# Where attention scores and gating stand in the instruction order of a hybrid encoder

## The chip, the core and the metric

The kernel runs on one core of one Trainium2 chip. A core has engines that each run their own instructions in order: TensorE (PE in the profile, its weight loads PEld), VectorE (DVE), ScalarE (ACT), GpSimd (POOL) and SyncE (SP, which here issues most of the weight transfers). An instruction that waits holds up all that stands behind it on its engine. The metric is the device time of one execution in microseconds (us), as the median of several runs.

## The reference

Two layers (DEPTH = 2) on 256 tokens with 1024 channels, all in float32. Each layer normalises x, projects it once into all its inputs, and runs two mixers next to each other:

```python
for l in range(DEPTH):
    h = rmsnorm(x, norm_w[l])
    proj = h @ w_in[l]
    (q_a, k_a, v_a, ab_a, z_a, q_b, k_b, v_b, z_b,
     gate_a, gate_b) = jnp.split(proj, SPLIT_IDX, axis=-1)
    y_a = gated_delta_branch(q_a, k_a, v_a, ab_a, z_a, ...)
    y_b = diff_attention_branch(q_b, k_b, v_b, z_b, cos, sin, ...)
    merged = (jax.nn.sigmoid(gate_a) * (y_a @ w_pa[l])
              + jax.nn.sigmoid(gate_b) * (y_b @ w_pb[l]))
    x = x + merged @ w_out[l]
return rmsnorm(x, final_norm_w)
```

Branch b is differential attention with 8 heads. Each head has two sets of queries and keys of 64 channels. Two softmaxes p[0] and p[1] are taken, `a = p[0] - lam * p[1]` is multiplied by v, the result is normalised by its root mean square, weighted and multiplied by `silu(z_b)`. Branch a is a gated delta rule that runs over the tokens in both directions, in chunks: it needs a small triangular system solved for each chunk and head, and passes a state from chunk to chunk. Its output is normalised and gated by `silu(z_a)`.

## The kernel before

**Products.** Every product of the 256 tokens with a weight matrix is made in pieces of 512 columns. The weights come from HBM in four transfers of 512 KB per piece (index kp, 256 rows each; tile `raw_<name>`). ScalarE rounds each to a high part (`hi_<name>`, line 251), and VectorE subtracts to get the low part (`lo_<name>`, line 253). These two steps are called casts here. TensorE then makes three matmuls per 128 rows of weights (index kt, 0 to 7) and token half: high by high, high by low, low by high (lines 266 to 268). So a kt is 6 matmuls, and a piece 48. There are two buffers each for the high and the low part and three for the raw weights, so a cast can run only when TensorE is done with the cast two before it.

**Stages of a layer.** First v_b, then the convolved k, q and v of branch a, the q and k of branch b (`qk`), then the pieces zb0, zb1, za0, za1 (z of the two branches), gb0, gb1, ga0, ga1 (the merge gates), pb0, pb1 (branch b's output projection), pa0, pa1 and the output. Other work is put between these products:

- During zb0 to za1, the attention heads 0 to 7. `scores(h, after)` makes for each of two query tiles (qt) and two halves (n = 1, then n = 0) one product of 64 rows by 256 columns (line 913; in fp32, so two matmul instructions each, tile `sc`). The half n = 0 reads rows 0 to 63, n = 1 rows 64 to 127. Each half has its own PSUM bank; heads 2 to 7 share the two banks of one pool. VectorE takes the maxima (`mx`, line 920), ScalarE the exponentials (`es`, line 922), and VectorE combines the two softmaxes (lines 925 to 928). `attend(h, es, at, after)` transposes the result on TensorE (tile `at`, line 939) and multiplies by v (tile `av`, line 946). It gets its own two pins. On VectorE the same stretch holds `substitute`, the solution of the triangular systems step by step (lines 722 and 723), which is pinned to casts.
- During gb0 and gb1, the last head's attention, four products of keys and queries with their weighing by decays (`weigh_q`: `kq` on TensorE, line 653, then line 685 on VectorE), and the first merges of the triangular blocks (lines 775 to 821).
- After gb's casts are traced: the scales of branch b's output (`rb`, with a power on GpSimd, line 157) and `gated` for branch b. For four blocks (column piece i, token half m) `gated` makes four multiplications on VectorE (line 1026) and then transposes and splits the block (`split_T`; tile `pt_yb`, then `ybT`), which is the input of pb.
- During ga and pb, `chunks`, the passing of the state: `ktm` is scaled on VectorE (line 850), then products `sp`, `ks`, `y2p`, `qs`, `po`. `key_sums` (lines 888 to 899) sums the squares of the queries, with a way through DRAM, behind the last weighing.

**Order.** The order of the instructions on each engine is drawn up by a scheduler with a model of the times, not by the order of the source. It takes what is ready, by priority. What the source adds are pins: inside `with behind(x)` each instruction that runs on the same engine as x is queued after x. That is an order of issue alone, not a wait for x to end. In `scores` only the first product (qt = 0, n = 1) is pinned; the other three are kept behind it in program order. The pins of TensorE are given as places, a running count of kt over the pieces: 0 to 7 in zb0, 8 to 15 in zb1, 16 to 23 in za0, 24 to 31 in za1, 32 to 39 in gb0, 40 to 47 in gb1, 48 to 55 in ga0, 56 to 63 in ga1:

```python
names = [f"{nm}{l}{i}" for nm in ("zb", "za", "gb", "ga", "pb") for i in range(2)]
place = lambda at: mark["done", names[at // KT], at % KT]
```

So `place(5)` is the last matmul of zb0's sixth kt. `mark[name, kp]` holds the two casts of a piece's transfer, high and low; `[1]` is the low one, on VectorE.

Of the kernel before, what the change touches and what calls it, by code (L numbers as in the profile page):

```python
# [12 lines left out]
ALU = mybir.AluOpType  # L13
# [4 lines left out]
P = 128  # L18
# [3 lines left out]
NM = SEQ // P  # L22
# [27 lines left out]
def hybrid_encoder(  # L50
# [53 lines left out]
    mark = {}  # L104
# [45 lines left out]
    def heads4(ap):  # L150
        return ap.rearrange("p (h e) -> p h e", e=P)
# [72 lines left out]
    def behind(ins):  # L224
        return nullcontext() if ins is None else tc.issue_after(ins)
# [138 lines left out]
    for l in range(DEPTH):  # L364
# [463 lines left out]
        def chunks(g):  # L828

            U = U_[:, g]  # L830
            h0 = 4 * g
            hs4 = slice(h0, h0 + 4)

            def four(nm, lhs, rhs):
                ps = (bank if g else bank_c)(f"{nm}{l}{g}")
                for j4 in range(4):
                    with behind(mark["pin"]):
                        T.matmul(ps[:, j4 * P : (j4 + 1) * P], lhs(j4), rhs(j4), start=True, stop=True)
                return ps

            y1 = [A[:, g, d] for d in range(2)]
            st = [ktm[:, d, hs4, :] for d in range(2)]
            y2 = [vtm[:, 1 - d, hs4, :] for d in range(2)]
            for d in range(2):
                ps = four(f"y1p{d}", lambda j: U[:, tix(d, d, j), :], lambda j: vtm[:, d, h0 + j, :])
                S.copy(flat(y1[d]), ps)
            yield
            for d in range(2):
                with behind(mark[f"gb{l}1", 1][1]):
                    V.tensor_tensor(st[d], st[d], last(kds[:, d, hs4], P), ALU.mult)  # L850
                ps = four(f"sp{d}", lambda j: st[d][:, j, :], lambda j: y1[d][:, j, :])
                S.copy(flat(st[d]), ps)
            yield
            for d in range(2):
                cs = 1 - d
                ps = four(f"ks{d}", lambda j: kq[:, h0 + j, cs, 0, :], lambda j: st[d][:, j, :])
                for j4 in range(4):
                    V.scalar_tensor_tensor(y2[d][:, j4, :], ps[:, j4 * P : (j4 + 1) * P],
                                           nE[:, 2 * d + cs, h0 + j4 : h0 + j4 + 1],
                                           y2[d][:, j4, :], ALU.mult, ALU.add)  # L860
            yield
            for d in range(2):
                cs = 1 - d
                ps = four(f"y2p{d}", lambda j: U[:, tix(d, cs, j), :], lambda j: y2[d][:, j, :])
                S.copy(flat(y2[d]), ps)
                ps = four(f"qs{d}", lambda j: kq[:, h0 + j, cs, 1, :], lambda j: st[d][:, j, :])
                for j4 in range(4):
                    S.activation(osb(g, cs)[:, j4, :], ps[:, j4 * P : (j4 + 1) * P], AF.Copy,
                                 scale=E_[:, 2 * d + cs, h0 + j4 : h0 + j4 + 1])
                yield  # L870
            for c in range(NM):
                po = (bank if g else bank_c)(f"po{l}{g}{c}")
                for j4 in range(4):
                    for d in range(2):
                        yy = y1[d] if d == c else y2[d]
                        with behind(mark["pin"]):
                            T.matmul(po[:, j4 * P : (j4 + 1) * P], B[:, c, h0 + j4, d, :], yy[:, j4, :],
                                     start=d == 0, stop=d == 1)
                V.tensor_tensor(osb(g, c), heads4(po), osb(g, c), ALU.add)
                yield  # L880
# [51 lines left out]
        def attend(h, es, at, after):  # L932
            with tc.high_priority(offset=HP):
                ap_ = bank(f"at{l}{h}")
                aT = work.tile([P, NM, SEQ], F32, tag="w2a", name=f"aT{l}{h}", bufs=2)
                for qt in range(NM):
                    for kt in range(NM):
                        with behind(at):
                            T.transpose(ap_[:, kt * SEQ + qt * P : kt * SEQ + (qt + 1) * P],
                                        es[:, 0, qt, kt * P : (kt + 1) * P], ident)  # L940
                S.copy(aT.rearrange("p k q -> p (k q)"), ap_)
                op_ = bank(f"av{l}{h}")
                for qt in range(NM):
                    for kt in range(NM):
                        with behind(after):
                            T.matmul(op_[:, qt * P : (qt + 1) * P], aT[:, kt, qt * P : (qt + 1) * P],
                                     vb[h // 4][:, kt, h % 4 * P : h % 4 * P + P],
                                     start=kt == 0, stop=kt == NM - 1)
            oh = ob[h // 4][:, :, h % 4 * P : h % 4 * P + P]
            S.copy(oh, op_[:, :SEQ].rearrange("p (q e) -> p q e", q=NM))  # L950
            for qt in range(NM):
                S.activation(sqj[:, :P], oh[:, qt, :], AF.Square, accum_out=ssb[:, qt, h : h + 1])
# [50 lines left out]
        for p in range(4):  # L1003
            z_part((zb, za)[p // 2], (C_ZB, C_ZA)[p // 2], ("zb", "za")[p // 2], p % 2)
            for h in (2 * p, 2 * p + 1):
                es[h] = scores(h, place(4 * h))
                if h:
                    attend(h - 1, es[h - 1], place(4 * h + 1), place(4 * h + 3))
            substitute(names[p])
            if p == 0:  # L1010
                place_v(mark[f"zb{l}0", 0][0])
                place_v(mark[f"zb{l}0", 3][0])
            elif p == 1:
                place_v(mark[f"zb{l}1", 1][0])
# [3 lines left out]
        step(mg)  # L1018
        step(mg)

        def gated(o_, z_, r_, nw_, yT, nm, tiles=range(NM)):
            for i in range(2):
                for m in tiles:
                    zv, ov = heads4(z_[i][:, m, :]), o_(i, m)
                    for j in range(4):
                        V.scalar_tensor_tensor(ov[:, j, :], ov[:, j, :],
                                               r_[:, m, 4 * i + j : 4 * i + j + 1],
                                               zv[:, j, :], ALU.mult, ALU.mult)
                    split_T(yT[i], ov, m, f"{nm}{i}", w=nw_)

        def gate(c_base, nm, tag, between=(None, None)):
# [9 lines left out]
        def branch(yT, w_, gt, nm, places=(None,) * 4):  # L1041
            for i in range(2):
                def evac_p(m, ps, i=i):
# [3 lines left out]

        gtb = gate(C_GB, f"gb{l}", "ev",
                   (lambda: attend(7, es[7], place(33), place(35)),
                    lambda: [weigh_q(n // 2, n % 2, place((36, 38, 40, 41)[n])) for n in range(4)]))  # L1050
        r0 = small.tile([P, NM, NH], F32, tag="r0", name=f"r0{l}")
        V.reciprocal(r0, s_all[:, :, 0, :].rearrange("p h q -> p q h"))
        rb = small.tile([P, NM, NH], F32, tag="rb", name=f"rb{l}")
# [3 lines left out]
        V.scalar_tensor_tensor(rb, rb, 0.5 * (1.0 - lam0), r0, ALU.mult, ALU.mult)  # L1057

        ybT = pair(f"ybT{l}")
        gated(lambda i, m: heads4(ob[i][:, m, :]), zb, rb, nw[:, 1:2], ybT, f"yb{l}")  # L1060

        gta = gate(C_GA, f"ga{l}", "eo")
        branch(ybT, w_pb[l], gtb, f"pb{l}")
# [110 lines left out]
```

## Time and profile before

| what | us |
|---|---|
| median of 3 runs (772.15 to 773.23) | 772.15 |
| the profiled execution, its whole time | 775.43 |
| its span, first to last instruction | 773.7 |

The profile is of one execution. Its rows count from the span's start. An engine's busy time is the union of its instructions; matmuls overlap, and their ends are modelled, so the distance from one start to the next says more than a duration. The granted TensorE clock was 0.998 of full speed over the span. A row of the timeline or of a group of instructions gives the engine, the line in the kernel, the operation, the tiles written and read, the shapes and the count; what stands in square brackets is the idle time of the engine before it and who ended it. A row of the chain of waits gives start, duration, engine, tile and line of a piece of the chain that ended last.

### The profile page before, as it was taken

What the parts mean: (1) busy time and instruction counts of PE and PEld (TensorE: products, weight loads), DVE (VectorE), ACT (ScalarE), POOL (GpSimd) and SP (SyncE); (2) the same over time, 40 slices, a digit from 0 to 9 for tenths busy, and PEclk for the clock granted to TensorE, in tenths of its full rate; (3) what the DMA queues carried; (4) which work ended last, traced back from release to release, by engine and by line L of the source; (5) the groups of instructions that cost most, each with busy time, mean ns of one, the idle gap of its engine ahead of it and who ended that gap; (6) DMA issues with size and microseconds to landing.
All of it is one profiled execution on the core that took longest, in us unless ns stands there. A gap on an engine that the chain in (4) does not pass through costs nothing.

```text
span 773.7 us, 13772 instructions
## 1 busy us (share of the span) xinstructions
PE 756.6 (98%) x5158; PEld 643.9 (83%) x5158; DVE 577.7 (75%) x1083; ACT 471.9 (61%) x1012; POOL 125.9 (16%) x187
## 2 busy tenths in 40 slices
PE   7999999999999999999999999999999999999996
PEld 4899889977778789988889889888677878998884
DVE  5686899989876754487567779999989685527782
ACT  5657675567765664655545677555777746465541
POOL 5000441111123011000010025202110410301000
PEclk9999999999999999999999999999999999999999
DMA  7662767765469542356674258768554965323641
GB/s 238 219 188 71 223 196 209 224 183 177 126 193 219 168 137 87 108 161 226 212 224 137 83 148 262 206 178 235 158 164 116 218 212 166 112 83 110 218 136 54
DMA packets 71794, 131.24 MB, mean 170 GB/s; under 512 B 12287, under 2 KB 12751, under 8 KB 71728
## 3 DMA queue, kind: packets, MB, share of 16 engines
q1 hardware_dynamic: 62718, 111.94, 48.4%
q0 software_dynamic: 6304, 15.15, 7.4%
q10 hardware_dynamic: 2706, 3.28, 1.3%
q8 instruction: 40, 0.66, 0.4%
q14 instruction: 26, 0.21, 0.1%
HBM read 123.44 MB, written 6.91 MB: 168 GB/s over the span
## 4 chain that ended last, share of the span: by engine, by line
PE 75%; DVE 10%; DMA 9%; ACT 3%; issue 2%; POOL 1%; SPq 0%; POOLq 0%; DVEq 0%; ACTq 0%
PE pp_vb L306 4%; PE sc L913 3%; DMA raw_gb<-in_w_in_dram 2%; PE pp_qk L267 2%; PE pp_qk L268 2%; DMA raw_vb<-in_w_in_dram 2%; PE pp_qk L266 2%; PE pp_o L306 2%; PE pf_v L322 2%; PE pp_za L267 2%; PE pf_v L326 2%; PE pf_v L324 2%; PE pp_ga L268 2%; PE pp_ga L266 2%; PE pf_k L322 2%
## 5 line engine op out<-in xcount | busy, mean ns | idle before, releaser
L267 PE MATMUL pp_qk<-lo_qk,hT 128*128 128x512 f32 x128 | 50.7, 396 | 0.3
L268 PE MATMUL pp_qk<-hi_qk,hT 128*128 128x512 f32 x128 | 50.0, 391 | 0.0
L253 DVE TENSOR_TENSOR lo_qk<-raw_qk,hi_qk 128x1024 fp32r<-128x1024 f32 x32 | 39.8, 1243 | 9.7 <-ACT hi_qk L251 9.5
L251 ACT CAST hi_qk<-raw_qk 128x1024 fp32r<-128x1024 f32 x28 | 29.4, 1050 | 25.9 <-PE pp_qk L268 12.6
L266 PE MATMUL pp_qk<-hi_qk,hT 128*128 128x512 f32 x128 | 45.2, 393 | 0.0
L253 DVE TENSOR_TENSOR lo_pb<-raw_pb,hi_pb 128x1024 fp32r<-128x1024 f32 x16 | 19.6, 1224 | 26.3 <-ACT hi_pb L251 26.1
L324 PE MATMUL pf_q<-hT,hi_q 128*128 128x256 f32 x128 | 36.2, 286 | 0.0
L322 PE MATMUL pf_q<-hT,hi_q 128*128 128x256 f32 x128 | 36.1, 287 | 0.0
L322 PE MATMUL pf_v<-hT,hi_v 128*128 128x256 f32 x128 | 35.9, 285 | 0.0
L324 PE MATMUL pf_v<-hT,hi_v 128*128 128x256 f32 x128 | 35.8, 284 | 0.0
L322 PE MATMUL pf_k<-hT,hi_k 128*128 128x256 f32 x128 | 35.8, 285 | 0.0
L324 PE MATMUL pf_k<-hT,hi_k 128*128 128x256 f32 x128 | 35.7, 283 | 0.0
L326 PE MATMUL pf_q<-hT,lo_q 128*128 128x256 f32 x128 | 34.9, 285 | 0.0
L922 ACT ACTIVATE es<-sc,mx 128x256 f32<-128x256 f32 x64 | 29.7, 475 | 8.2 <-DVE mx L920 8.2
L326 PE MATMUL pf_v<-hT,lo_v 128*128 128x256 f32 x128 | 34.5, 288 | 0.0
L326 PE MATMUL pf_k<-hT,lo_k 128*128 128x256 f32 x128 | 34.3, 283 | 0.0
L551 DVE SCALAR_TENSOR_TENSOR cvq<-pf_q,cw,cvq 128x254 f32<-128x254 f32 (+1 forms) x64 | 29.9, 476 | 1.9 <-ACT cvq L547 1.4
L251 ACT CAST hi_pa<-raw_pa 128x1024 fp32r<-128x1024 f32 x16 | 16.9, 1054 | 23.2 <-PE pp_pa L268 17.0
L551 DVE SCALAR_TENSOR_TENSOR cvv<-pf_v,cw,cvv 128x254 f32<-128x254 f32 (+1 forms) x64 | 30.0, 480 | 0.1
L551 DVE SCALAR_TENSOR_TENSOR cvk<-pf_k,cw,cvk 128x254 f32<-128x254 f32 (+1 forms) x64 | 28.5, 479 | 2.0 <-ACT cvk L547 1.3
L267 PEld LDWEIGHTS pp_qk<-lo_qk,hT 128*128 128x128 f32 x128 | 24.0, 188 | 6.8 <-DVE lo_qk L253 2.0
L253 DVE TENSOR_TENSOR lo_ga<-raw_ga,hi_ga 128x1024 fp32r<-128x1024 f32 x16 | 19.4, 1223 | 12.7 <-ACT hi_ga L251 12.7
(362 smaller groups left out, 2525.4 us busy)
## 6 DMA issues: line engine op xcount, KB each, us to landing
raw_qk<-in_w_in_dram SPq DMA_DIRECT2D x32, 512.0 KB, 4.0
raw_k<-in_w_in_dram SPq DMA_DIRECT2D x16, 512.0 KB, 4.6
raw_q<-in_w_in_dram SPq DMA_DIRECT2D x16, 512.0 KB, 3.7
raw_v<-in_w_in_dram SPq DMA_DIRECT2D x16, 512.0 KB, 3.7
raw_zb<-in_w_in_dram SPq DMA_DIRECT2D x16, 512.0 KB, 3.8
raw_za<-in_w_in_dram SPq DMA_DIRECT2D x16, 512.0 KB, 3.7
raw_gb<-in_w_in_dram SPq DMA_DIRECT2D x16, 512.0 KB, 5.3
raw_o<-in_w_out_dram SPq DMA_DIRECT2D x16, 512.0 KB, 4.9
```

The costliest lines, as they stand in the source:

```text
L251: high = (V.tensor_copy if kp in turned else S.copy)(hi[:, :, :n], raw[:, :, :n]).ins
L253: mark[nm, kp] = high, V.tensor_tensor(lo[:, :, :n], raw[:, :, :n], hi[:, :, :n].bitcast(F32), ALU.subtract).ins
L266: T.matmul(o, act[kt // 4][:, 0, kt % 4, ts_], hi, start=kt == 0, stop=False)
L267: T.matmul(o, act[kt // 4][:, 0, kt % 4, ts_], lo, start=False, stop=False)
L268: mark["proj"] = T.matmul(o, act[kt // 4][:, 1, kt % 4, ts_], hi, start=False, stop=kt == KT - 1).ins
L306: mark["proj"] = T.matmul(o, a_, w_, start=kt == 0 and a_ is ah and w_ is hi, stop=kt == KT - 1 and a_ is al).ins
L322: T.matmul(o, hi[:, cs], act[kt // 4][:, 0, kt % 4, :], start=first, stop=False, skip_group_check=True)
L324: T.matmul(o, hi[:, cs], act[kt // 4][:, 1, kt % 4, :], start=False, stop=False, skip_group_check=True)
L326: T.matmul(o, lo[:, cs], act[kt // 4][:, 0, kt % 4, :], start=False, stop=done, skip_group_check=True)
L551: V.scalar_tensor_tensor(ca[:, o0:o1], acc[:, b, o0 + sft : o1 + sft], cw[:, j, cb : cb + 1], ca[:, o0:o1], ALU.mult, ALU.add)
L913: mm = T.matmul(sp[n][:, qt * SEQ : (qt + 1) * SEQ], qkT[h // 4][rows, 0, h % 4, qt * P : (qt + 1) * P], qkT[h // 4][rows, 1, h % 4, :], s ...
L922: S.activation(es[:, n, qt, :], spv[:, qt, :], AF.Exp, bias=mx[:, n, qt : qt + 1], accum_out=s_all[:, h, n, qt : qt + 1])
```

## The change

No instruction is added or removed. Four sets of pins change:

1. Scores of the heads 0 to 7: from the places 0, 4, 8, ..., 28 to 2, 6, 12, 15, 19, the last matmul of head 3's attention product (for head 5), that of head 4's (for head 6), and 31. To be able to name them, `attend` now records its last matmul in `mark["av", h]`.
2. `weigh_q`: from the places 36, 38, 40, 41 to 37, 41, 43, 45.
3. The scaling of `ktm` in `chunks(g)`: from behind the low cast of gb1's second transfer to behind the low cast of ga0's transfer g (0 or 1).
4. The gating of branch b, unpinned before: its four blocks go behind the low casts 1, 2, 3 and 3 of gb1. The pin holds the multiplications alone, not the transposes and splits after them. Branch a's gating, which uses the same function, stays unpinned.

```diff
@@ chunks
-                with behind(mark[f"gb{l}1", 1][1]):
+                with behind(mark[f"ga{l}0", g][1]):
                     V.tensor_tensor(st[d], st[d], last(kds[:, d, hs4], P), ALU.mult)
@@ attend
-                            T.matmul(op_[:, qt * P : (qt + 1) * P], aT[:, kt, qt * P : (qt + 1) * P],
+                            mark["av", h] = T.matmul(op_[:, qt * P : (qt + 1) * P], aT[:, kt, qt * P : (qt + 1) * P],
                                      vb[h // 4][:, kt, h % 4 * P : h % 4 * P + P],
-                                     start=kt == 0, stop=kt == NM - 1)
+                                     start=kt == 0, stop=kt == NM - 1).ins
@@ the z products
-                es[h] = scores(h, place(4 * h))
+                es[h] = scores(h, mark["av", h - 2] if h in (5, 6) else place((2, 6, 12, 15, 19, 0, 0, 31)[h]))
                 if h:
                     attend(h - 1, es[h - 1], place(4 * h + 1), place(4 * h + 3))
@@ gated
-        def gated(o_, z_, r_, nw_, yT, nm, tiles=range(NM)):
+        def gated(o_, z_, r_, nw_, yT, nm, tiles=range(NM), after={}):
...
-                        V.scalar_tensor_tensor(ov[:, j, :], ov[:, j, :],
-                                               r_[:, m, 4 * i + j : 4 * i + j + 1],
-                                               zv[:, j, :], ALU.mult, ALU.mult)
+                        with behind(after.get((i, m))):
+                            V.scalar_tensor_tensor(ov[:, j, :], ov[:, j, :],
+                                                   r_[:, m, 4 * i + j : 4 * i + j + 1],
+                                                   zv[:, j, :], ALU.mult, ALU.mult)
@@ gate gb
-                    lambda: [weigh_q(n // 2, n % 2, place((36, 38, 40, 41)[n])) for n in range(4)]))
+                    lambda: [weigh_q(n // 2, n % 2, place((37, 41, 43, 45)[n])) for n in range(4)]))
@@ the gating of branch b
-        gated(lambda i, m: heads4(ob[i][:, m, :]), zb, rb, nw[:, 1:2], ybT, f"yb{l}")
+        gated(lambda i, m: heads4(ob[i][:, m, :]), zb, rb, nw[:, 1:2], ybT, f"yb{l}",
+              after={(i, m): mark[f"gb{l}1", min(2 * i + m + 1, 3)][1] for i in range(2) for m in range(NM)})
```

## The prediction, made before the change was run

> **What bounds the kernel now.** I read the page first, then the chain of waits, then the timeline of the two stages in which the pins move.
>
> ```profile
> span 773.7 us, 13772 instructions
> PE 756.6 (98%) x5158; PEld 643.9 (83%) x5158; DVE 577.7 (75%) x1083; ACT 471.9 (61%) x1012; POOL 125.9 (16%) x187
> ```
>
> TensorE is the bound: it is idle for 773.7 - 756.6 = 17 us in all, and no instruction is added or taken away. A gain can come from two places only: from matmuls that take longer than they must (a busy PE row hides that), and from the idle time. So I looked for both where the diff moves work.
>
> The first is in the scores. These are the rows of the chain of waits (start, duration) for the z products of layer 1, with the attention products that stand next to them:
>
> ```profile
> 172.69 0.63 PE sc L913 x2
> ...
> 175.33 1.06 PE sc L913 x6
> ...
> 182.91 0.63 PE sc L913 x2
> ...
> 186.49 1.06 PE sc L913 x6
> ...
> 194.12 0.63 PE sc L913 x2
> ...
> 203.86 1.06 PE sc L913 x8
> ...
> 208.73 0.63 PE sc L913 x2
> ...
> 211.86 0.89 PE av L946 x8
> 212.75 1.06 PE sc L913 x6
> ...
> 219.43 0.89 PE av L946 x8
> 220.32 0.63 PE sc L913 x2
> ...
> 227.35 0.63 PE sc L913 x2
> ```
>
> A head has eight score matmuls: two query tiles, two halves n, each an fp32 product of two instructions. The halves use rows 64 to 127 and 0 to 63 of the array, and run side by side when they are issued together: head 4, in one piece, takes 1.06 us for eight. Where the first pair (n = 1 of query tile 0, the one that is pinned) is issued alone, it has no partner: 0.63 us for two, and the six that follow later take 1.06 all the same, since their last pair is alone too. Seven of eight heads are split like this, in both layers; a split costs **0.63 us** of TensorE.
>
> The second is a pair of waits in the product gb, for the low half of its weights:
>
> ```profile
>   PEld pp_gb L267: 3.2, 4
>   PE pp_gb L267: 1.9, 4
> ```
>
> These are the rows "who waited" of tile raw_gb: four waits, two in each layer, 1.9 us of idle PE (3.2 by its weight loads, which stop first).
>
> **Scores, head by head.** A pin cannot move a head to an earlier place, only hold its first pair back; the other six stay behind it. So I compare the new pin with where the two parts are now, counting the product's matmuls (six to a place).
>
> Head 1: first pair after place 4, the rest after 38 matmuls of zb0; new pin 42. Head 2: first pair after 62, rest after 74 of zb; new pin 78. Head 5: rest directly behind head 3's attention product at 211.86, which is the new pin. Head 7: rest after 92 of za, new pin 96. In these four the pin lies at or just behind the point at which the second part went out, so its PSUM bank is free by then and all eight go out together: 4 x 0.63 = 2.5 us per layer. Head 4's pin (24 matmuls of za) is where it stands now: 0. Head 3's (96 of zb) and head 6's (behind head 4's attention) are where their first pairs stand already, at 194.12 and 220.32; I take 0 for both, bounds 0 and -0.63 each.
>
> Head 0 is different. It merges too, but its two parts cost nothing today:
>
> ```profile
> 165.44 1.04 ACT L251 CAST hi_zb<-raw_zb 128x1024 fp32r<-128x1024 f32 x1
> ...
> 165.59 0.70 PE L913 MATMUL sc<-qkT 64*128 64x256 f32 x2
> ...
> 166.53 0.73 PE L266 MATMUL pp_zb<-hi_zb,hT 128*128 128x512 f32 x2 [0.25 <-ACT hi_zb L251]
> ...
> 166.76 1.22 DVE L253 TENSOR_TENSOR lo_zb<-raw_zb,hi_zb 128x1024 fp32r<-128x1024 f32 x1
> ...
> 167.19 1.13 PE L913 MATMUL sc<-qkT 64*128 64x256 f32 x6
> ...
> 168.25 0.50 PE L267 MATMUL pp_zb<-lo_zb,hT 128*128 128x512 f32 x1
> ```
>
> PE waits here for zb0's second pair of k-tiles: the high half ends at 166.48, the low half at 167.98. The scores fill both waits. Held back to place 2 (the third k-tile) they leave them empty: the low product can start some 0.2 us sooner, and then 1.06 + about 0.1 for the change of shape comes on top. I take **+0.9 us** per layer; bounds +1.2 (nothing gained at 168) and -0.6 (the scheduler finds other work for the gap).
>
> Together 0.9 - 2.5 = -1.6 us per layer, -3.2 for both. The later scores delay each head's softmax. That costs nothing while its transposes find products to run beside; every head has a z or gb product over it.
>
> **Gating, ktm and kq.** The same two waits in the timeline of layer 1:
>
> ```profile
> 242.49 2.94 POOL L157 TENSOR_TENSOR rb<-rspre,mhalf 128x16 f32<-128x16 f32 x1
> ...
> 247.71 0.17 DVE L1057 SCALAR_TENSOR_TENSOR rb<-rb,r 128x16 f32<-128x16 f32 x1
> ...
> 248.83 1.05 ACT L251 CAST hi_gb<-raw_gb 128x1024 fp32r<-128x1024 f32 x1 [1.77 <-DMA raw_gb<-in_w_in_dram]
> 248.93 3.76 DVE L1026 SCALAR_TENSOR_TENSOR ob<-ob,rb,zb 128x128 f32<-128x128 f32 x14
> ...
> 253.12 1.23 DVE L253 TENSOR_TENSOR lo_gb<-raw_gb,hi_gb 128x1024 fp32r<-128x1024 f32 x1
> ...
> 254.26 2.50 DVE L850 TENSOR_TENSOR ktm<-ktm,kds 128x512 f32<-128x512 f32 x4
> ...
> 254.40 0.50 PE L267 MATMUL pp_gb<-lo_gb,hT 128*128 128x512 f32 x1 [0.67 <-DVE lo_gb L253]
> ...
> 258.93 2.36 DVE L253 TENSOR_TENSOR lo_gb<-raw_gb,hi_gb 128x1024 fp32r<-128x1024 f32 x2
> ...
> 260.21 0.50 PE L267 MATMUL pp_gb<-lo_gb,hT 128*128 128x512 f32 x1 [0.47 <-DVE lo_gb L253]
> ```
>
> VectorE runs the 16 gatings in one block ahead of gb1's second cast, and the ktm scaling (4 instructions, 2.50 us) and two kq weighings ahead of the third and fourth. With the gatings queued behind casts 1, 2, 3 and 3 and ktm behind ga's casts, the casts go first and both waits go: -1.9 us for the layers together (bounds 0 and -3.2). What the moved work feeds comes later: gating feeds ybT, which pb reads when ga is done; ktm feeds this:
>
> ```profile
> L838 PE MATMUL sp<-A,ktm x32: 270/275/275, 286.3 to 290.2; 128*128 128x128 f32 x32
> ```
>
> From 256.8, the scaling's end, to 286.3 there are 29 us of cover. Head 7, now behind all of za, gives rb later than 247.88, by 2 to 3 us as an estimate (its own eight matmuls and the last four of za). The first gating is now behind the second cast of gb1, which can run from 249.88 to 251.1, when its high half is there; so VectorE has no wait for rb that PE would see. The kq groups keep their size, later by one to four places, each followed by its weighing on VectorE:
>
> ```profile
> 242.14 1.23 DVE L685 TENSOR_TENSOR B<-kq,B 128x1024 f32<-128x1024 f32 x1 [0.15 <-PE kq L653]
> ```
>
> One group (eight matmuls of the shape that takes 0.89 us in the av rows above) leaves the stretch before gb1 and head 7's scores (1.06) enter it, so PE reaches gb1's first cast no sooner than now. I take 0.
>
> **Sum.** -3.2 - 1.9 = -5.1 us. The profiled execution took 775.43 us (span 773.7), so 770.3 on its scale; it lies 3.3 above the median of the runs, 772.15, so **767.0 us** there. The forecast's own range: with heads 3 and 6 merged (-2.5) and all of the 3.2 waits gone, 772.15 - 8.9 = 763.2; with two merges, head 0 at 1.2 and half of the waits, about 771.
>
> **Rivals.** *Evacuation holds the gain* (0.15). Two banks of scores now land at once, and the maxima over them wait on VectorE:
>
> ```profile
> 170.00:178.00 8.00, 8.00 (x40) 5.74 (x39) 8.00 (x20) 6.08 (x17) 2.31 (x5) 1.00 0.65 206
> 178.00:186.00 8.00, 8.00 (x37) 6.22 (x36) 8.00 (x18) 6.60 (x17) 0.42 (x1) 1.00 0.59 173
> ...
> 262.00:266.00 4.00, 4.00 (x57) 3.34 (x48) 1.05 (x2) 3.30 (x7) 0.00 (x0) 1.00 0.66 238
> ```
>
> (Busy us of PE, weight loads, VectorE, ScalarE, POOL.) VectorE is full for 16 us from 170 on, so PE saved there could turn into waits for low halves. Then the merges give nothing, head 0 costs 1.8 and gb returns 1.9: 772 us, no change. Against it: in that stretch head 0 puts PE behind, not ahead. [...]
>
> *Key sums come late and block VectorE* (0.17), the slower side. They wait for the last kq weighing, now at gb1's sixth k-tile, and stand behind the gatings and ktm:
>
> ```profile
> 283.45 2.20 POOL L898 DMA_DIRECT2D qss<-qdr  x4 [1.46 <-DMA qdr<-qss]
> ...
> 289.02 0.26 DVE L899 TENSOR_REDUCE ssq<-qss 128x16 f32<-128x64 f32 x1 [5.37 <-DMA qss<-qdr]
> ...
> 293.44 0.17 DVE L1084 TENSOR_TENSOR rq<-rq 128x16 f32<-128x16 f32 x1 [2.82 <-POOL rq L1082]
> 294.16 1.12 DVE L858 SCALAR_TENSOR_TENSOR vtm<-ks,nE,vtm 128x128 f32<-128x128 f32 x4 [0.54 <-PE ks L838]
> ```
>
> VectorE already stands still for 5.37 us for that DMA and 2.82 us for POOL, and the updates of vtm, for which the chunk chain on PE waits, come 0.5 us behind. A shift of s us costs PE s - 0.5 per layer. From s = 3.1 it eats the whole gain (2 x 2.6 = 5.2); with s = 5, 767.0 + 9.0 = 776; with 4, 774. For it: 4.3 us of gating (16 x 0.27), 2.5 of ktm and two weighings of 1.23 move towards it. Against: from 262 to 266 VectorE is busy for 1.05 of 4 us, so there is room for them.
>
> *All splits go* (0.08): heads 3 and 6 merge and head 0 is hidden: 2 x 7 x 0.63 + 1.9 = 10.7, 761.4 us.
>
> **How the numbers follow.** Forecast 0.60, of which 0.06 is within 0.2% (about 1.5 us, what a measurement can tell here). Faster: 0.54 + 0.08 + 0.03 of the first rival = 0.65; same: 0.06 + 0.11 = 0.17; slower: 0.17 + 0.01 = 0.18. The range 763 to 775 holds the forecast, the first rival and the slower one up to s = 4.5, and leaves out most of the last.
>
> **What would show it.** Right: the chain of waits has score pieces of x8 at 1.06 for heads 1, 2, 5 and 7 and no x2 of 0.63 there; PE idles about 1.5 us at zb0's second cast; tile raw_gb has no wait of PE at L267; the maxima (L920) and exponentials (L922) keep their busy time. Wrong: x2 pieces still in number; new idle time of PE at L939, L946 or L838; the wait at L899 ends later relative to the ks products. What would break the forecast is the order of the instructions itself: the scheduler draws it anew for all engines, and a pin of a few matmuls can move work that the diff doesn't name.

## The result, and the profile after

The changed kernel takes **768.0 us** (median of 7 runs, 767.3 to 771.1), the kernel before 772.71 beside it (7 runs, 771.5 to 775.4): a ratio of 0.9947, 95% interval 0.9925 to 0.9969. That is 4.7 us less; 767.0 was forecast. Its profiled execution took 769.31 us. The tables below compare one execution of each kernel; that of before (775.43) lies 2.7 us above this median, that of after 1.3, so they differ by 6.1 us where the medians differ by 4.7.

The head of its page, beside the one shown of before (span 773.7, PE busy 756.6):

```profile
span 767.5 us, 13772 instructions
PE 748.7 (98%) x5158; PEld 640.6 (83%) x5158; DVE 576.9 (75%) x1083; ACT 470.1 (61%) x1012; POOL 125.8 (16%) x187
```

PE is busy 7.9 us less and idle 18.8 us instead of 17.1. To see where, both traces are cut at the same events: zb0's first matmul, gb0's first, gb1's last, ga1's last. The first three rows are layer 1, the others layer 2. The columns are busy us of PE, weight loads, VectorE, ScalarE, POOL, then the granted clock, DMA share and GB/s. Before:

```profile
162.70:232.00 69.30, 69.05 (x342) 51.89 (x342) 60.35 (x130) 50.36 (x138) 10.43 (x18) 1.00 0.57 163
232.00:266.60 34.60, 33.45 (x477) 27.75 (x476) 24.75 (x44) 20.88 (x47) 7.44 (x11) 1.00 0.80 200
266.60:310.00 43.40, 43.40 (x377) 38.81 (x376) 21.62 (x39) 26.05 (x48) 6.68 (x6) 1.00 0.38 115
539.80:609.60 69.80, 69.00 (x341) 51.86 (x340) 60.23 (x130) 50.43 (x138) 9.74 (x17) 1.00 0.57 162
609.60:644.00 34.40, 33.66 (x477) 27.86 (x476) 24.73 (x44) 20.98 (x47) 8.13 (x12) 1.00 0.80 200
644.00:687.40 43.40, 43.40 (x377) 38.82 (x376) 21.21 (x38) 25.77 (x47) 6.66 (x6) 1.00 0.36 113
```

After:

```profile
162.20:228.80 66.60, 64.28 (x338) 49.38 (x336) 59.52 (x129) 50.14 (x137) 8.61 (x16) 1.00 0.56 160
228.80:262.80 34.00, 33.02 (x473) 27.47 (x472) 21.54 (x39) 19.08 (x46) 10.22 (x13) 1.00 0.88 211
262.80:307.10 44.30, 44.30 (x386) 39.65 (x385) 25.27 (x45) 27.36 (x50) 5.76 (x6) 1.00 0.39 121
536.00:601.30 65.30, 63.97 (x338) 49.42 (x336) 59.42 (x129) 49.45 (x135) 9.16 (x16) 1.00 0.56 163
601.30:637.00 35.70, 34.41 (x473) 28.69 (x472) 21.71 (x39) 19.14 (x46) 9.69 (x13) 0.95 0.85 204
637.00:681.30 44.30, 44.30 (x386) 39.68 (x386) 24.77 (x44) 27.12 (x49) 5.76 (x6) 1.00 0.38 115
```

The z products are 2.7 and 4.5 us shorter, together 7.2, more than twice what the forecast had (3.2). The gate products give some of it back: gb and ga together were 78.0 and 77.8 us and are 78.3 and 80.0, so they lost 2.5 us where the forecast had them win 1.9. ga is longer by 0.9 and 0.8 because eight transposes of the gated output (`pt_yb`) moved there out of gb in each layer; gb in turn took in four transposes of head 6 (`at`), which stood at the end of z before and take 0.45 us where the chain of waits has four of them. The remaining 1.5 us of the span lie outside these windows.

**The scores.** The chain of waits of the kernel after, through zb and za of layer 1:

```profile
190.03 1.06 PE sc L913 x8
195.42 1.06 PE sc L913 x8
...
203.46 1.06 PE sc L913 x8
...
219.10 1.06 PE sc L913 x8
```

Not one piece of 0.63 is left: all eight heads of a layer go out in one piece, heads 3 (195.42) and 6 (219.10) too, whose pins had not seemed to move anything. PE's busy time in z falls by 4.8 and 5.0 us: seven splits at 0.63 are 4.4, and head 6's transposes are 0.45. The windows also show what it costs: PE's idle time in z is 2.3 and 1.3 us, before 0.25 and 0.8. In layer 1 most of it is at zb0's second cast, where head 0 used to stand (timeline of after):

```profile
165.69 0.73 PE L266 MATMUL pp_zb<-hi_zb,hT 128*128 128x512 f32 x2 [0.62 <-ACT hi_zb L251]
...
167.19 0.50 PE L267 MATMUL pp_zb<-lo_zb,hT 128*128 128x512 f32 x1 [0.76 <-DVE lo_zb L253]
...
168.32 1.13 PE L913 MATMUL sc<-qkT 64*128 64x256 f32 x8
...
187.94 1.16 PE L946 MATMUL av<-vb,aT 128*128 128x128 f32 x8 [0.67 <-ACT aT L941]
```

In layer 2 PE waits only 0.39 us there. The last row is a wait that came with the new order, for ScalarE's copy of head 1's transposed attention weights; in layer 2 it is 0.68 us.

**The gate products.** The rows of tile `raw_gb`, the raw weights of gb, for the kernel after: what its instructions waited for (in part), then which PE rows waited for them (us, times), then the time from issue to landing.

```profile
  DMA raw_gb<-in_w_in_dram: 11.6, 2
...
  PE pp_gb L267: 1.7, 3
...
  PE pp_gb L266: 0.5, 1
...
DMA to landing us min/median/max: 3.8/7.8/13.3
```

Before, PE waited 1.9 us at L267, and the landings were:

```profile
DMA to landing us min/median/max: 3.6/5.3/10.8
```

So the waits that were to go are still there, 2.2 us of them. But they are other waits. These are rows of the timeline of layer 1, all engines, first of the kernel before:

```profile
233.29 0.50 ACT L922 ACTIVATE es<-sc,mx 128x256 f32<-128x256 f32 x1
...
233.74 1.08 ACT L251 CAST hi_gb<-raw_gb 128x1024 fp32r<-128x1024 f32 x1
...
236.22 0.39 SPq L247 DMA_DIRECT2D raw_gb<-in_w_in_dram  x1
...
245.48 1.05 ACT L251 CAST hi_gb<-raw_gb 128x1024 fp32r<-128x1024 f32 x1 [3.92 <-DMA raw_gb<-in_w_in_dram]
```

And of the kernel after:

```profile
227.79 1.04 ACT L251 CAST hi_gb<-raw_gb 128x1024 fp32r<-128x1024 f32 x1
...
230.12 1.71 SPq L247 DMA_DIRECT2D raw_gb<-in_w_in_dram  x1
...
230.73 0.47 ACT L922 ACTIVATE es<-sc,mx 128x256 f32<-128x256 f32 x1 [0.42 <-DVE mx L920]
...
240.45 0.83 PE L946 MATMUL av<-vb,aT 128*128 128x128 f32 x6
243.48 1.04 ACT L251 CAST hi_gb<-raw_gb 128x1024 fp32r<-128x1024 f32 x1 [5.43 <-DMA raw_gb<-in_w_in_dram]
244.43 0.36 ACT L950 COPY ob<-av 128x256 f32<-128x256 f32 x1
...
245.83 0.50 PE L267 MATMUL pp_gb<-lo_gb,hT 128*128 128x512 f32 x1 [0.44 <-DVE lo_gb L253]
...
251.65 0.18 DVE L1058 SCALAR_TENSOR_TENSOR rb<-rb,r 128x16 f32<-128x16 f32 x1 [3.13 <-POOL rb L157]
...
255.32 0.50 PE L267 MATMUL pp_gb<-lo_gb,hT 128*128 128x512 f32 x1 [0.53 <-DVE lo_gb L253]
```

In the kernel before, gb0's second cast stands on ScalarE behind head 7's exponentials (233.29, then 233.74). Its low half frees the buffer for gb1's first transfer, which is issued at 236.22 and has landed by 245.48, 9.3 us later. In the kernel after, head 7 comes later and the cast stands ahead of its exponentials, so the transfer is issued 6.1 us earlier, at 230.12. But its high cast cannot start before 243.48, 13.3 us later.

Two things are late now. The transfer makes PE wait for the low half at 245.83. And behind that cast, in ScalarE's queue, stands head 7's copy: its product was finished at 241.28 (240.45 + 0.83), the copy starts 3.15 us later. On the copy hang the sums of squares, POOL's power and `rb`, which VectorE has at 251.65 instead of 247.71. VectorE stands still 3.13 us for it, with the first gatings and the third low half behind, and PE waits for that half at 255.32. In layer 2 the late first transfer costs more: PE waits 0.53 us for its high half and 0.76 for its low one, and then the granted clock is at half from 619.35 to 622.76, for 3.41 us (windows of 2 us, PE's busy time first, the clock behind POOL):

```profile
618.00:620.00 2.00, 1.24 (x3) 0.83 (x4) 2.00 (x2) 1.86 (x7) 0.00 (x0) 0.84 0.71 256
620.00:622.00 2.00, 2.00 (x7) 1.52 (x6) 1.83 (x4) 1.73 (x4) 1.17 (x1) 0.50 0.81 220
```

The starts of PE's products are 0.43 us apart there (620.24 to 621.09), and 0.23 at full clock (614.33 to 615.69). So the 3.41 us at half clock are worth another 1.7 us, as an estimate (half of them).

### The profile page after: what moved, and what is told of

The parts are those of the page before. It is cut to its first block, busy times and chain, and to the rows that moved or that the text cites. A ratio compares the mean times of both kernels' runs of the same rounds, so it can differ in the third digit from the quotient of the medians.

```text
span 767.5 us, 13772 instructions
## 1 busy us (share of the span) xinstructions
PE 748.7 (98%) x5158; PEld 640.6 (83%) x5158; DVE 576.9 (75%) x1083; ACT 470.1 (61%) x1012; POOL 125.8 (16%) x187
## 4 chain that ended last, share of the span: by engine, by line
PE 74%; DVE 12%; DMA 7%; ACT 3%; issue 2%; POOL 1%; POOLq 0%; ACTq 0%; DVEq 0%
PE pp_vb L306 5%; DMA raw_gb<-in_w_in_dram 4%; PE pp_qk L267 2%; PE pp_qk L268 2%; PE pp_qk L266 2%; PE pp_o L306 2%; PE pf_v L322 2%; PE pf_k L322 2%; PE pf_v L326 2%; PE pf_k L324 2%; PE pf_k L326 2%; PE pf_v L324 2%; PE pp_za L266 2%; PE pp_za L267 2%; DMA raw_qk<-in_w_in_dram 2%
## 5 line engine op out<-in xcount | busy, mean ns | idle before, releaser
L267 PE MATMUL pp_qk<-lo_qk,hT 128*128 128x512 f32 x128 | 50.8, 397 | 0.4 <-DVE lo_qk L253 0.2
L253 DVE TENSOR_TENSOR lo_gb<-raw_gb,hi_gb 128x1024 fp32r<-128x1024 f32 x16 | 19.5, 1221 | 18.1 <-ACT hi_gb L251 17.9
L267 PEld LDWEIGHTS pp_qk<-lo_qk,hT 128*128 128x128 f32 x128 | 24.0, 188 | 7.2 <-DVE lo_qk L253 2.4
```

What stands on the lines that cost most here:

```text
L253: mark[nm, kp] = high, V.tensor_tensor(lo[:, :, :n], raw[:, :, :n], hi[:, :, :n].bitcast(F32), ALU.subtract).ins
L267: T.matmul(o, act[kt // 4][:, 0, kt % 4, ts_], lo, start=False, stop=False)
```

## The experiments

Each ratio is against runs of the kernel before on the same chip, with its 95% interval. In this section "after" is the changed kernel, 0.9947.

**The parts alone.** `s_only` has only the scores' pins (part 1), `rest_only` only the kq, ktm and gating pins (parts 2 to 4).

```diff
# s_only, on before
-                es[h] = scores(h, place(4 * h))
+                es[h] = scores(h, mark["av", h - 2] if h in (5, 6) else place((2, 6, 12, 15, 19, 0, 0, 31)[h]))
# rest_only, on after
-                es[h] = scores(h, mark["av", h - 2] if h in (5, 6) else place((2, 6, 12, 15, 19, 0, 0, 31)[h]))
+                es[h] = scores(h, place(4 * h))
```

> The pins of the scores alone, with kq, ktm and gating as before. Theory (the merged scores carry the gain): all eight heads of a layer go out as x8 at 1.06 us, each z stage is about 2.2 us shorter, and gb keeps its two waits for low halves in each layer; ratio to before 0.993 to 0.996. Rival (the other pins are needed for it): the saved time comes back as waits in gb, ratio 0.998 or more.

> The pins of kq, ktm and gating alone, with the scores as before. Theory of the forecast: the casts of gb1 go ahead of the gating, the 1.9 us of idle PE at L267 of gb go, ratio about 0.9975. Rival (what bounds gb1 is the landing of its first transfer of weights, 13.26 us after its issue in the changed kernel, and not the gating): the wait only moves to the first cast of gb1, ratio 0.9995 to 1.001.

Measured: `s_only` 771.81 us, ratio 0.9998 [0.9984, 1.0013]; `rest_only` 771.01, 0.9986 [0.9974, 0.9997]. Added they are 0.16% less, together they make 0.53%. `s_only` gains in z as after does (66.8 and 66.0 us), but gb and ga together take most of it back (78.9 and 81.7 us, before 78.0 and 77.8). In layer 2 head 7's copy stands behind gb1's late first cast, and a kq product of PE behind the copy (ScalarE's timeline, then PE's):

```profile
619.25 1.04 ACT L251 CAST hi_gb<-raw_gb 128x1024 fp32r<-128x1024 f32 x1 [5.49 <-DMA raw_gb<-in_w_in_dram]
...
620.62 1.44 PE L653 MATMUL kq<-kq 128*128 128x128 f32 x8 [1.82 <-ACT ob L950]
```

`rest_only` shows what gb can be: 32.0 us, no idle PE. Its z products take nearly as long as before (68.8 us in each layer), its ga 0.8 longer. The window of gb in layer 1:

```profile
232.10:264.10 32.00, 32.00 (x469) 27.04 (x468) 21.44 (x39) 19.66 (x45) 7.36 (x11) 1.00 0.88 215
```

So the waits at L267 do go by parts 2 to 4, as the forecast said, as long as the scores stand where they stood: gb1's first transfer is issued at 236.37 here, as late as before. The 0.9975 of its theory lies within the interval. Its profiled span, though, is 5.1 us shorter than that of before (768.6 against 773.7), while the medians differ by 1.4; how much of this is due to the execution of before that was profiled, above its median, is not known.

**Head 0 back to place 0**, in after.

```diff
-place((2, 6, 12, 15, 19, 0, 0, 31)[h])
+place((0, 6, 12, 15, 19, 0, 0, 31)[h])
```

> The changed kernel with head 0 alone pinned to place 0 again. Theory (its two parts fill PE's wait for zb0's second cast for nothing): head 0 is split again as 0.63 + 1.06 us, PE's idle 0.78 + 0.93 us there is filled, about 0.65 us less per layer, so 1.3 us below the changed kernel: ratio to before about 0.993. Rival (VectorE, full for 16 us there, takes it back): ratio as the changed kernel's, 0.9947.

Measured: 771.04 us, ratio 0.9981 [0.9963, 0.9999]: no gain, and by the medians a loss of 3 us against after, though the two intervals overlap. The pin of head 0 alone redraws the order of later heads; heads 3, 4 and 5 are split again, with pieces of two at 193.31, 201.35 and 212.50 (chain of waits):

```profile
193.31 0.63 PE sc L913 x2
```

What head 0 costs by itself cannot be read from the time of this run. At its own place, the two parts fill PE's wait for zb0's second cast again: PE idles 0.5 us in z of layer 1, where it is 2.3 in after. The run does show that the merges of the other heads hang on head 0's place as well as on their own.

**What holds gb1's first transfer.** Two edits of after, each of the order of transfers alone. `raw_o_late` queues the two early transfers of the output's weights (`raw_o`) behind gb1's last; `t_pool` has POOL issue the four loads of T that SP issues right ahead of gb1's first transfer. T and U are the blocks of the triangular system, in pieces of 128 bytes.

```diff
# raw_o_late (it also records each transfer in mark, not shown)
-                with behind(load):
+                with behind(load or (mark.get(('raw', f'gb{nm[1]}1', 3)) if nm[0] + nm[2:] == 'o0' and kp in spare else None)):
# t_pool
-                (nc.sync if g else G).dma_start(out=T64[blk(b), :, co : co + 32],
+                G.dma_start(out=T64[blk(b), :, co : co + 32],
```

> The changed kernel with the two early transfers of the output weights (raw_o) queued on SyncE behind the last transfer of gb1; nothing else moves. Theory (they share the DMA engines with gb1's first transfer and make it land late): it lands 2.5 to 5 us sooner than 13.26 us after its issue, PE's wait at gb1's first cast (0.72 us in layer 1, 1.75 in layer 2, and some 2 us of half clock behind that) goes; 1 to 4 us below the changed kernel, ratio to before 0.990 to 0.993. Rival (the small-piece loads of U and T hold it): landing as now, ratio 0.9947.

> The kernel after, with the four loads of T of the second merge group issued by POOL instead of SP; they are then no longer on the queue ahead of gb1's first weight transfer, and nothing else is moved. Theory A (those small-piece loads, right ahead of it on the same queue, hold gb1's first weight transfer): its landing time falls from 13.3 us to about 10 or less, PE's waits for gb1's first casts (1.5 us in layer 1, 1.75 in layer 2) and the half clock behind them in layer 2 go, 2 to 4 us less than after, ratio 0.990 to 0.993. Rival B (the DMA engines are simply full at that time, whoever issues): landing stays above 12 us, waits stay, ratio 0.9947 as after.

Measured: `raw_o_late` 768.89 us, ratio 0.9945 [0.9928, 0.9963], longest landing 14.0 us: `raw_o` is not the cause. `t_pool` 774.03, 1.0011 [0.9995, 1.0027]. There gb1's first transfer lands after 9.9 us (issued at 231.27), the longest landing falls to 11.0, and no wait of PE for gb's casts is left, so theory A was right in that. But T, now queued on POOL behind U's loads, is late itself:

```profile
247.29 1.02 PE L775 MATMUL y64p<-T,A 32*32 32x32 f32 x86 [2.10 <-DMA T<-udr]
```

That wait takes the place of the others. Its profiled span is 3.1 us over that of after, the median 6. Half clock is part of that difference: the granted clock of the profiled execution is 0.994, that of most others 0.991 to 0.993, and 3.41 us at half clock are 0.002 of the span. The rest is not known.

**The kq pins and the gating pins, each undone** in after.

```diff
# no_kq
-place((37, 41, 43, 45)[n])
+place((36, 38, 40, 41)[n])
# no_gate
-        gated(lambda i, m: heads4(ob[i][:, m, :]), zb, rb, nw[:, 1:2], ybT, f"yb{l}",
-              after={(i, m): mark[f"gb{l}1", min(2 * i + m + 1, 3)][1] for i in range(2) for m in range(NM)})
+        gated(lambda i, m: heads4(ob[i][:, m, :]), zb, rb, nw[:, 1:2], ybT, f"yb{l}")
```

> The kernel after, with the four kq groups back at places 36, 38, 40, 41. Theory A (the kq pins are what makes the score merges pay: at its old place a kq product waits for head 7's copy, which stands on ScalarE behind gb1's late first cast): a wait of PE at a kq product of 1 to 2 us with a lower clock behind it comes back in at least one layer, ratio 0.997 to 1.000. Rival B (the kq pins are worth nothing by themselves): ratio 0.9947 as after, no wait of PE at kq.

> The kernel after, with the gatings of the attention output not held behind gb1's casts (ktm stays behind ga's first casts). Theory A (the block of 16 gatings on VectorE ahead of gb1's low halves is what made PE wait at L267): the waits at L267 for gb grow from 1.7 us in the two layers by 1 to 3 us, ratio 0.996 to 0.999. Rival B (after the change gb1's casts wait for the transfer, so that the gatings would fill a stretch in which VectorE is idle anyway): waits as in after, ratio 0.9947 give or take 0.001.

Measured: `no_kq` 768.13 us, ratio 0.9937 [0.9919, 0.9955], so the kq pins are worth nothing in time and theory A fell. Its wait does come back in layer 1, without a lower clock to be seen (0.998 over the span, as in the kernel before), but it only stands in place of the two at the low halves (0.44 and 0.53 us in after), of which none is left (PE's timeline):

```profile
245.20 1.16 PE L653 MATMUL kq<-kq 128*128 128x128 f32 x8 [0.94 <-ACT ob L950]
```

`no_gate` 776.72 us, ratio 1.0054 [1.0033, 1.0074]: the gating pins are worth some 8 us in the new order (after has 0.9947), far beyond the 1 to 3 that even theory A gave them. VectorE's timeline and PE's, layer 1:

```profile
251.04 4.29 DVE L1027 SCALAR_TENSOR_TENSOR ob<-ob,rb,zb 128x128 f32<-128x128 f32 x16
...
256.38 1.22 DVE L253 TENSOR_TENSOR lo_gb<-raw_gb,hi_gb 128x1024 fp32r<-128x1024 f32 x1
...
257.65 0.50 PE L267 MATMUL pp_gb<-lo_gb,hT 128*128 128x512 f32 x1 [3.17 <-DVE lo_gb L253]
```

All 16 gatings stand in one block ahead of a low half, as they did before: there gb1's second, here its third. But before, `rb` was there at 247.71 and the block ran from 248.93 on. With head 7 late it runs from 251.04 on, when PE is already one transfer further. PE's waits at L267 come to 7.4 us in the two layers, and half clock follows both (granted clock 0.50 from 260 to 262 and from 636 to 640).

**The two halves of the scores.** In after, all four instructions of half n = 1 ahead of the four of n = 0.

```diff
-            for qt in range(NM):
-                for n in (1, 0):
+            for n in (1, 0):
+                for qt in range(NM):
```

> The kernel after, with the two loops of the scores exchanged: both query tiles of half n = 1, then both of n = 0; the same eight instructions, no longer alternating between the two halves of the array's rows. Theory A (two halves run side by side when issued in turn, and a split lost that): eight take 1.7 to 2.3 us instead of 1.06, 16 heads by 0.65 to 1.2 us, 10 to 19 us more than after, ratio 1.008 to 1.02. Rival B (a split only costs filling and draining at a change of shape, the rest is indifferent to the order): eight take 1.0 to 1.2 us as before, ratio 0.9947 give or take 0.002.

Measured: 771.98 us, ratio 0.9986 [0.9971, 1.0002]. Both theories miss something. The heads in one piece still take 1.07 us (chain of waits; 1.06 in after), so the order within the eight makes 0.01 us. But two heads in each layer were split by the new order, one of them in this way (PE's timeline):

```profile
203.23 1.13 PE L913 MATMUL sc<-qkT 64*128 64x256 f32 x4
...
205.15 1.13 PE L913 MATMUL sc<-qkT 64*128 64x256 f32 x4
```

Four instructions of one half alone last as long as eight of both (1.13 us at 189.96 in after; 1.06 for either in the chain of waits). With x2 at 0.63 and x6 at 1.06 one sum fits all the pieces measured: 0.21 us for each instruction of the half that has more of them, and 0.21 on top. So the halves do run side by side in both orders of issue measured, where nothing else comes between.

**Two causes, one edit each.** `ob_first` is after with gb1's first cast behind head 7's copy and sums on ScalarE; the order on TensorE, POOL and SyncE stays as it is, but on VectorE the cast's low half falls behind a weighing and the sums of `ssb` as well. `tub1` has T's loads on POOL where U's stood, and U's on SP behind gb1's second transfer. `ob_tub1` has both.

```diff
# ob_first
-                S.activation(sqj[:, :P], oh[:, qt, :], AF.Square, accum_out=ssb[:, qt, h : h + 1])
+                mark["sq", h] = S.activation(sqj[:, :P], oh[:, qt, :], AF.Square, accum_out=ssb[:, qt, h : h + 1]).ins
-                proj_tm(hT, wl, c_base + 512 * i, 512, evac_g, f"{nm}{i}", between=between[i])
+                proj_tm(hT, wl, c_base + 512 * i, 512, evac_g, f"{nm}{i}", between=between[i],
+                        later={0: (mark["sq", 7], None)} if i and tag == "ev" else None)
# tub1, loads of U, with their step moved behind gb (T's loads as in t_pool, for both groups)
-                G.dma_start(out=U_[blk(b), :, :, blk(b)].rearrange("j g t i -> j (g t) i"),
+                with behind(mark["raw", f"gb{l}1", 1]):
+                    nc.sync.dma_start(out=U_[blk(b), :, :, blk(b)].rearrange("j g t i -> j (g t) i"),
```

> The kernel after, with one pin more, on ScalarE alone: gb1's first cast behind head 7's copy and its two sums of squares. Nothing is moved on TensorE, VectorE, POOL or SP. Theory A (after, head 7's copy stands 3.15 us in ScalarE's queue behind that cast, which waits for its transfer; so rb comes late, VectorE stands still for it with the first gatings, and the third low half of gb1 comes late): the copy starts at about 241.3 instead of 244.4 in layer 1, rb some 3 us earlier, VectorE's wait of 3.13 us for rb shrinks to under 0.5, PE's wait of 0.78 us at that low half goes; 0.8 to 2 us less than after, ratio 0.992 to 0.994. Rival B (the wait at that low half comes from the late transfer, not from rb): the wait stays, ratio 0.9945 as after.

> The kernel after, with the loads of T of both merge groups on POOL, where U's stood, and U's loads on SP behind gb1's second weight transfer: the same bytes, but the small-piece loads of U start some 6 us later and none stands ahead of gb1's first transfer. Theory A (the small-piece loads of T and U that start within 6 us of it hold gb1's first transfer): its landing falls from 13.3 us to under 11, PE's waits at gb1's first cast (0.72 us in layer 1, 1.75 in layer 2) and the half clock behind them go, the wait for T that cost 2 us when T stood behind U does not come; 2 to 4 us less than after, ratio 0.990 to 0.993. Rival B (U's loads at their new place hold gb1's second and third transfers instead): the waits move to gb1's later casts or to the products with U, ratio 0.9945 to 0.998.

> Both edits of ob_first and tub1 together. Theory A (two causes, the late transfer and the late rb, each with waits of its own): the gains add, gb as long as without waits (31.9 us per layer), 3 to 5 us less than after, ratio 0.988 to 0.991. Rival B (they are one cause: with the transfer on time the copy is no longer held): as tub1 alone.

Measured: `ob_first` 766.98 us, ratio 0.9934 [0.9917, 0.9951]; `tub1` 766.74, 0.9934 [0.9916, 0.9951]; `ob_tub1` 765.96, 0.9923 [0.9904, 0.9942]. All three are faster than the kernel before; that they are faster than after, by 1 to 2 us, is not clear of the intervals, but the traces show waits gone at the places named. In `ob_first` the copy of layer 1 starts with its product's end, VectorE does not wait for `rb`, and PE does not wait in gb:

```profile
241.34 0.37 ACT L950 COPY ob<-av 128x256 f32<-128x256 f32 x1 [3.27 <-PE av L946]
...
247.62 0.17 DVE L1059 SCALAR_TENSOR_TENSOR rb<-rb,r 128x16 f32<-128x16 f32 x1
```

In layer 2 PE still waits for gb1's first cast (0.54 and 0.76 us). In `tub1` no row of PE is left among those who waited for `raw_gb`, and its landings are:

```profile
DMA to landing us min/median/max: 3.5/6.3/7.7
```

So the small-piece loads are what held gb1's first transfer: 13.3 us in after, 9.9 with T off SP's queue (`t_pool`), 6.3 here, where U's loads start 8 us later as well (236.08 against 228.00; longest landing 7.7). T's loads alone, on POOL, do not hold it: they start beside it here too (226.93 to 232.12, the transfer at 230.45). With it on time, head 7's copy is on time as well: one late transfer is behind both waits in layer 1. In that, rival B of `ob_tub1` was right; its gains do not add (PE even waits 0.64 us for a low half in layer 1 there), and the tenth of a per cent by which its median lies below that of `tub1` is not told apart.

**Scores and gatings alone**: parts 1 and 4, with kq and ktm as before.

```diff
-place((37, 41, 43, 45)[n])
+place((36, 38, 40, 41)[n])
-                with behind(mark[f"ga{l}0", g][1]):
+                with behind(mark[f"gb{l}1", 1][1]):
```

> The scores' pins and the gating's pins alone: kq back at its four old places and ktm back behind gb1's second low half, all else as after. Theory A (the two that need each other are the scores and the gatings; kq and ktm are worth nothing): ratio 0.993 to 0.996, as after and as no_kq, with ktm's 2.5 us in the stretch in which VectorE waits for rb. Rival B (ktm's four scalings on VectorE ahead of gb1's third low half hold it up, since rb comes late): a longer wait of PE at that low half in both layers, ratio 0.997 to 0.999.

Measured: 772.05 us, ratio 1.0 [0.9985, 1.0015]: theory A fell, since this and `no_kq` (0.9937) differ only in ktm's pin. But it is not as rival B had it either: no wait of PE for that low half is left, only 0.42 and 0.60 us for head 7's copy, ahead of a kq product. The time is in the order on PE, where kq's products now alternate with the small `zt` products:

```profile
252.98 0.24 PE L789 MATMUL zt<-U__96,y 32*32 32x32 f32 x2
253.15 0.49 PE L653 MATMUL kq<-kq 128*128 128x128 f32 x2
...
255.35 0.66 PE L789 MATMUL zt<-U__96,y 32*32 32x32 f32 x54
```

From 252.98 to 255.35, 2.4 us go by for 8 kq products that take 0.8 us in one piece in `no_kq` (251.47 to 252.27) and 8 small ones. This place is 1.5 us or so, and layer 2 has the same one (627.93 to 630.29), so together they make 3 of the 3.9 us between the two kernels. That ktm's pin, on VectorE, moves products on PE is put down to the scheduler, which places all engines together; no run tests it.

## Why the prediction was right, and where its steps were wrong

The time, 4.7 us less against a forecast of 5.1, came out near by luck: in the windows z gained 7.2 us where 3.2 was forecast, the gate products lost 2.5 where they were to win 1.9, and the two errors cancel.

- **Scores, mechanism right, count wrong.** A split does cost 0.63 us, by the sum that fits the pieces in `unpaired`. The step "Head 3's ... and head 6's ... are where their first pairs stand already ... I take 0 for both" failed: heads 3 and 6 merged as well. Beside head 0 that is six merges, not four, 3.8 us per layer instead of 2.5. z also lost head 6's transposes to gb (0.45) and took in new waits of 0.9 per layer, 0.7 at head 1's `av` and 0.2 at a low half, which were not foreseen. `h0_back` shows why a comparison head by head could not see it: whether a head is split depends on the whole order, and so on the pins of other heads.
- **Head 0, right in layer 1 only.** PE idles where the forecast said, 0.62 + 0.76 us by the waits shown, against "about 1.5"; in layer 2 it is 0.39. From zb0's first matmul to its seventh high product (line 266), head 0's scores included, after takes 0.6 us more than before in layer 1 (7.19 against 6.55) and 1.2 us less in layer 2 (5.92 against 7.14), where PE in the kernel before waited 0.55 us for `stg` ahead of these scores. The +0.9 per layer was read off layer 1 and taken for both; it came to about -0.6 in all.
- **Gating, right by itself, wrong in the sum.** "The casts go first and both waits go" holds in `rest_only`. With the scores in place it does not, because of two steps. "PE reaches gb1's first cast no sooner than now. I take 0" looked at PE's own work alone: gb0 started 3.2 us earlier (228.8 against 232.0), its second cast came 6 us earlier because head 7's exponentials no longer stood ahead of it, and gb1's first transfer with it (230.12 against 236.22). The loads of T and U, which follow the triangular solution on VectorE, moved by 1.4 us only (POOL's first load of U at 228.00 against 229.39). Before, the transfer was issued when all of them had been (POOL's last by 235.75); now it comes into the middle of them and takes 13.3 us to land. And "VectorE has no wait for rb that PE would see" is refuted by 3.13 us of VectorE ahead of the third low half. The lateness of `rb` was put at 2 to 3 us and was 3.9 (251.65 against 247.71); what was missed is that ScalarE holds head 7's copy behind a cast that waits for a transfer, and that the first gatings, pinned behind the second low half, are still ahead of the third.
- **kq and ktm.** "I take 0" for kq is borne out by the time of `no_kq`. ktm's pin was costed as a move of 2.50 us on VectorE under cover; its worth lies in the order of PE, which the sum had no term for.
- **The rivals.** Evacuation did not hold the gain: the maxima took 688 ns each before and 684 after, and PE's time did fall in that stage. Key sums did not block VectorE: the wait at L899 is 5.14 us where it was 5.37, and the sums come at 286.25 where they came at 289.02:

```profile
286.25 0.27 DVE L899 TENSOR_REDUCE ssq<-qss 128x16 f32<-128x64 f32 x1 [5.14 <-DMA qss<-qdr]
```

"All splits go" is what happened to the scores; its 761.4 was not reached because it, too, had both waits of gb gone, and head 0 hidden, where PE idles 2.3 and 1.3 us in z.

What stays open: how much of the change's worth is in its pins and how much in the one order that they happen to produce. `s_gate` and `h0_back` each change one thing and redraw much, so they bound no single part.

## What to carry to other kernels

When a stage is made shorter, look at what the next stage waits for and ask of each such transfer whether its start and its neighbours on the DMA engines move along; here gb1's first transfer moved by 6.1 us and the loads of T and U by 1.4, and its landing went from 9.3 us to 13.3. An instruction that waited for a transfer held what was queued behind it on its engine (here head 7's copy, by 3.15 us), so put short work that others need ahead of it. Under a scheduler that draws the order anew, the parts of this change did not add: 0.02% and 0.14% alone, 0.53% together, and a step costed part by part can be right in the sum by luck.

## What was not expected of the hardware

- Two row halves of TensorE ran side by side in both orders of issue measured: eight score instructions take 1.06 us alternating (after) and 1.07 with the four of one half first (`unpaired`); four of one half alone take 1.06 (203.30 and 205.22 in the chain of waits of `unpaired`).
- Waits of the same length came with half clock at one place and without it at others. In after, PE waits 0.53 and 0.76 us around gb1's first cast in layer 2 (618.00, 619.26) and the granted clock falls to 0.50 from 619.35 to 622.76; in `ob_first` it waits 0.54 and 0.76 at the same place (617.28, 618.54) and the clock stays at 1.00 (windows from 612 to 626). At zb0's second cast in layer 1 of after it waits 0.62 and 0.76 (165.69, 167.19), and the clock stays at 1.00 too (162.20 to 228.80). Half clock lasted 3.41 us in layer 2 of after, and in `no_gate` about 3.4 us in layer 1 and 6.8 in layer 2, an estimate from its granted clock in windows of 2 us (0.82, 0.50, 0.83 from 258 on; 0.69, 0.50, 0.50, 0.61 from 634 on). What decides whether the clock falls was not shown.
- With the DMA engines fully taken both times, the kernel after moved 173 GB/s from 234 to 238, while the small pieces of T and U were under way (share 1.15), and 358 GB/s from 242 to 246 (share 1.09). A full DMA share alone did not tell here how long a weight transfer takes.
